# The second MLP product of an encoder layer: a fourth of its seven inner products is itself split into seven, and the row differences that this needs are made where the rows are made

## The chip, the cores and the metric

The kernel runs on one core of one Trainium2 chip. The metric is the device time of one execution in microseconds (us); the lower the better. The times shown are those of several runs of the kernel; the profile is one more execution, recorded by the hardware profiler. The engines of the core are TensorE (PE; its weight loads are listed as PEld), VectorE (DVE), ScalarE (ACT), GpSimd (POOL) and SyncE (SP, which here issues nearly all DMAs).

## The reference

One layer of an encoder over 2048 rows of 1024 numbers, float32. Attention with an output projection comes first (its code is not touched here and is left out), then the MLP:

```python
x = x + gt1 * (mixed @ w_o[l])
h = rmsnorm(x, g_norm2[l]) * (1.0 + sc2) + sh2
x = x + gt2 * (jnp.square(jax.nn.relu(h @ w1[l])) @ w2[l])
```

`w1` is 1024 x 4096 and `w2` is 4096 x 1024. `gt2` is a vector over the 1024 columns, and the last line's result is the output.

## The kernel before

Everything is computed transposed: columns of the reference lie on the 128 partitions, rows of the sequence along the free axis, in four blocks of 512 (`TB`). Float32 products are made of three matmuls each (`mm3`): every operand is split into a high part, cast by ACT, and a low part, the remainder, subtracted by DVE (`operand`, `split`); high x high, high x low and low x high are added up in PSUM. So each operand tile costs an ACT cast and a DVE subtraction before PE can use it. Since one helper records PE's and SP's instructions in the order of the program, all lines of the profile carry its line, L42, and work is told apart by tile names.

**The MLP's products are split into seven.** Both matrices are cut into 2 x 2 blocks, and seven products of sums of blocks take the place of eight products of blocks (the Strassen-Winograd scheme). They are numbered 1, 6, 5, 7, 2, 3, 4; 1, 2 and 4 take blocks as they are, 5, 6, 3 and 7 sums and differences of blocks. The rows are worked on in two halves: `mb` 1 first, then `mb` 0, each with two blocks of 512 rows (`odd` 1 and 0).

**Steps.** The MLP is a list of steps (`steps`), run in order; a step issues its matmuls. Before step n runs, the jobs that were put down for n with `at(n, job)` are issued (loads, sums), and the operands of later steps are prepared as long as no more than 8 operand tiles are in use (`ready - used + nxt.tiles <= 8`). `later.add(k, job)` issues a job k steps later. DVE, ACT and POOL then take their instructions in an order that a scheduler makes of the program; PE's and SP's stay as written.

- `Mixed`: the last eight steps of the attention's output projection (tiles `pso`, weights `wo`), while the first four groups of MLP input rows (`right_blocks`, tiles `cy`, `h`) are normalised, summed and split by ACT and DVE.
- `First(mb, j, i)`, the first product: 16 pairs of hidden blocks j by seven products i, 12 matmuls a step. `fetch` makes the four sums of the weight tile `w1` of pair j (tiles `ts`, and one in place in `w`), on DVE. `run` ends with the four hidden blocks and the sums of them that the second product needs, and `keep(i, src)` stores each of the seven to DRAM (`scr_hid[mb, i, ...]`). The steps of `mb` 1 also make the sums of `w2` (`second_sums`, tiles `w2s`, kept in `scr_s`).
- `Second(mb, i, j)`, a *plain* product of the second matrix: products 1, 6, 5 and 7 (`PLAIN`), each for `mb` 1 and `mb` 0, in 16 steps of 12 matmuls into four PSUM banks (tiles `oph`, `opv`, both from `hw`). `out` gathers the results, and `update` adds them, times `gt2`, into the rows (`scr_x`; tiles `txu`, `cxu`).
- `Outer(i, q, k)`, a *doubled* product: products 2, 3 and 4 are each split once more into seven, over both halves `mb`, in 7 x 8 steps of 6 matmuls (tiles `opr`, `ol`, from `r` and `l`). The left sides are sums of `w2`, made by `outer_sums` during `First` of `mb` 0 and kept in `scr_t`. The right sides are the stored rows: `half` loads four of them (1, 5, 3, 2; 5 and 3 from `mb` 0, 1 and 2 from `mb` 1), and `half_sum` makes four sums on DVE (5, 6, 7, 4), in tiles of 128 x 1024. `end` adds a finished bank into rows `txo`, loaded by `load_x` one step into the inner product that needs them.

**Order of the tail before:** plain 1, plain 6, doubled 2, plain 5, doubled 3, plain 7, doubled 4, all for `mb` 0 where plain. `plan` says at which steps a doubled product's right sides are loaded and summed; these lie in the products ahead of it. Plain loads (`hw`) stand 7 steps ahead, those behind a doubled product up to 12.

The inner order of a doubled product is 1, 5, 6, 3, 7, 2, 4. The sixth (2) completes the rows of block "11" and the seventh (4) those of block "21"; the PSUM bank of the seventh is free when DVE has added it into its rows.

## Time and profile before

| | us |
|---|---|
| median of 3 runs | 2572.12 (2569.36 to 2574.5) |
| the profiled execution | 2573.75 |
| its span in the trace | 2572.0 |
| mean granted PE clock | 0.998 of full speed |

The stages of the MLP in the trace, with the columns PE, weight loads, DVE, ACT, POOL (busy us, number of instructions), granted clock, DMA share, GB/s: plain 1 and 6 of `mb` 0, doubled 2, plain 5, doubled 3, plain 7, doubled 4.

```profile
2161.00:2250.00 89.00, 89.00 (x394) 73.69 (x393) 65.69 (x91) 41.83 (x74) 0.00 (x0) 1.00 0.80 304
2250.00:2326.00 76.00, 75.53 (x334) 62.19 (x332) 68.74 (x105) 49.84 (x86) 0.00 (x0) 1.00 0.69 249
2326.00:2371.00 45.00, 44.38 (x196) 36.71 (x197) 33.63 (x47) 18.91 (x33) 0.00 (x0) 1.00 0.63 234
2371.00:2448.00 77.00, 75.69 (x334) 62.30 (x332) 70.36 (x107) 49.87 (x86) 0.00 (x0) 1.00 0.74 261
2448.00:2492.00 44.00, 43.55 (x192) 36.07 (x193) 35.13 (x50) 18.29 (x32) 0.00 (x0) 1.00 0.66 261
2492.00:2568.00 76.00, 75.85 (x332) 61.51 (x330) 62.87 (x100) 45.95 (x79) 0.00 (x0) 1.00 0.43 146
```

An instruction's row gives its start, its time, the engine, what it writes and reads, and in brackets how long the engine stood idle before it and what ended that. Such idle time matters only on the engine that sets the end.

### The profile page before, as it was taken

The numbers are of one execution on the slowest core, as the hardware profiler recorded it, in microseconds if no ns is written. First come the engines' busy times: TensorE is split into PE (matmuls) and PEld (weight loads), VectorE is DVE, ScalarE is ACT, GpSimd is POOL, SyncE is SP. The second block draws the span as 40 slices with busy tenths as digits, with TensorE's granted clock in tenths as the row PEclk, the third lists the DMA queues.
The fourth block names the chain that finished last, engine by engine and source line by source line (L and its number), as shares of the span: only waits on it lengthen the run. The fifth ranks groups of instructions, "written<-read, shape, count | busy, mean of one in ns | idle before, by whom it ended". The sixth has DMA issues, their size and how long they took to land.

```text
span 2572.0 us, 39296 instructions
## 1 busy us (share of the span) xinstructions
PE 2542.0 (99%) x12484; PEld 2115.9 (82%) x12484; DVE 1965.5 (76%) x3433; ACT 1483.7 (58%) x2849; POOL 747.3 (29%) x1128
## 2 busy tenths in 40 slices
PE   9999999999999999999999999999999999999999
PEld 7888888888888888887887888888888888888877
DVE  7656767887789879998767777678776765797987
ACT  6323435667866686666745555566455555464645
POOL 4330144776776667776610000000000000000000
PEclk9999999999999999999999999999999999999999
DMA  9879879788977788756786887787677866766763
GB/s 356 331 296 364 338 282 291 215 239 280 277 245 229 239 280 269 245 189 204 224 317 227 288 286 272 261 303 252 216 253 257 262 233 243 301 245 239 260 259 127
DMA packets 276943, 674.80 MB, mean 262 GB/s; under 512 B 29952, under 2 KB 75008, under 8 KB 266112
## 3 DMA queue, kind: packets, MB, share of 16 engines
q1 hardware_dynamic: 275440, 667.57, 75.7%
q10 hardware_dynamic: 1296, 4.72, 0.5%
q8 instruction: 99, 1.62, 0.3%
q14 instruction: 108, 0.88, 0.1%
HBM read 461.93 MB, written 210.24 MB: 261 GB/s over the span
## 4 chain that ended last, share of the span: by engine, by line
PE 85%; DVE 6%; DMA 3%; ACT 2%; issue 2%; POOL 1%; SPq 1%; DVEq 0%; POOLq 0%; ACTq 0%
PE ps L42 30%; PE ps_s L42 12%; PE pt L42 11%; PE acc L42 6%; PE wt L42 6%; PE po L42 4%; PE pf L42 4%; PE z L42 4%; PE pq L42 3%; PE cz L42 2%; DVE p L42 2%; PE pso L42 1%; DVE opr L42 1%; DMA txo<-scr_x 1%; PE ct L42 1%
## 5 line engine op out<-in xcount | busy, mean ns | idle before, releaser
L42 PE MATMUL ps<-h,opw 128*128 128x512 f32 x1512 | 358.6, 389 | 0.0
L42 ACT CAST wth<-wt 128x512 fp32r<-128x512 f32 (+3 forms) x544 | 257.5, 484 | 174.0 <-PE wt L42 164.0
L42 PE MATMUL ps<-oph,opv 128*128 128x512 f32 x1536 | 349.7, 389 | 2.9 <-DVE txo L42 2.9
L42 POOL TENSOR_TENSOR b<-p 128x512 f32<-128x512 f32 (+1 forms) x320 | 292.5, 914 | 167.9 <-DVE p L42 90.4
L42 PEld LDWEIGHTS ps<-oph,opv 128*128 128x128 f32 x1536 | 288.1, 188 | 63.8 <-DVE txo L42 3.7
L42 DVE TENSOR_TENSOR wtl<-wt,wth 128x512 fp32r<-128x512 f32 (+3 forms) x544 | 290.5, 545 | 59.6 <-ACT wth L42 57.1
L42 PEld LDWEIGHTS ps<-h,opw 128*128 128x128 f32 x1512 | 283.6, 188 | 58.9
L42 PE MATMUL pt<-w,ht 128*128 128x512 f32 x1248 | 288.2, 391 | 0.0
L42 PE MATMUL ps_s<-h,opw 128*128 128x512 f32 x1152 | 277.0, 389 | 0.0
L42 PEld LDWEIGHTS pt<-w,ht 128*128 128x128 f32 x1248 | 232.9, 188 | 47.7
L42 DVE TENSOR_TENSOR_SCAN p<-z,p,zero 128x512 f32<-128x512 f32 x192 | 245.6, 1280 | 25.8 <-ACT z L42 18.4
L42 PEld LDWEIGHTS ps_s<-h,opw 128*128 128x128 f32 x1152 | 216.1, 188 | 44.9
L42 PE MATMUL acc<-wth,v 128*128 128x512 f32 (+3 forms) x544 | 220.7, 410 | 0.0
L42 ACT ACTIVATE z<-z 128x512 f32<-128x512 f32 (+1 forms) x320 | 166.5, 521 | 55.2 <-PE z L42 49.3
L42 PE MATMUL z<-k,q 128*128 128x512 f32 (+3 forms) x640 | 185.6, 371 | 7.7 <-DVE p L42 7.2
L42 PE MATMUL acc<-wtl,v 128*128 128x512 f32 (+3 forms) x544 | 185.7, 348 | 0.0
L42 PE MATMUL wt<-ident,b 128*128 128x128 f32 x1088 | 171.4, 273 | 1.0 <-DVE cols L42 0.3
L42 PEld LDWEIGHTS wt<-ident,b 128*128 128x128 f32 x1088 | 136.3, 140 | 42.1 <-DVE cols L42 1.8
L42 POOL TENSOR_TENSOR e<-e,cols 128x640 f32<-128x640 f32 (+4 forms) x128 | 143.0, 1123 | 84.9 <-DVE cols L42 57.0
L42 PE MATMUL po<-fx,ow 128*128 128x512 f32 x576 | 161.7, 393 | 0.5 <-DMA ow<-scr_wo 0.5
L42 DVE TENSOR_TENSOR opw<-w,opw 128x512 fp32r<-128x512 f32 x127 | 87.3, 691 | 95.0 <-ACT opw L42 95.0
L42 ACT CAST opr<-r 128x512 fp32r<-128x512 f32 x168 | 104.4, 623 | 83.6 <-PE ps L42 46.9
(211 smaller groups left out, 4761.8 us busy)
## 6 DMA issues: line engine op xcount, KB each, us to landing
q<-scr_q SPq DMA_DIRECT2D x128, 256.0 KB, 4.9
w<-in_w_dram SPq DMA_DIRECT2D x64, 512.0 KB, 5.7
hw<-scr_hid SPq DMA_DIRECT2D x64, 512.0 KB, 6.2
k<-scr_k SPq DMA_DIRECT2D x240, 128.0 KB, 4.3
v<-scr_v SPq DMA_DIRECT2D x120, 256.0 KB, 4.1
wa<-in_w_ada_dram SPq DMA_DIRECT2D x48, 512.0 KB, 6.6
ow<-scr_wo SPq DMA_DIRECT2D x24, 1024.0 KB, 6.6
hw<-scr_s SPq DMA_DIRECT2D x48, 512.0 KB, 7.2
```

What stands on the lines that cost most here:

```text
L42: return lambda *x, **y: self.tc.keep_in_program_order(f(*x, **y))
```

## The change

1. Product 7 becomes a doubled product. `PLAIN` loses it, and a new list `DOUBLE` is (7, 2, 3, 4); `scr_t` and `outer_sums` get it as a fourth, the latter now over all 16 pairs j. The tail becomes plain 1, doubled 7, plain 6, doubled 2, plain 5, doubled 3, doubled 4. Product 7 enters two blocks of rows, so an `Outer` of it adds each finished bank into twice as many rows, and writes half of them back to `scr_x`.
2. The first of the four half sums (5) goes. Instead, in `First` of `mb` 0 and for j < 8, `other` loads the row of `mb` 1 that was stored before (tiles `to`, 128 x 512), `keep` subtracts it from the new row on DVE, and the difference is stored two steps later.
3. For `mb` 1 and j < 2, `fetch` makes its four sums on POOL instead of DVE.
4. `update` is rewritten for the rows that product 7 no longer completes, stores of `end` go through `later.add(2, ...)`, and the steps in `plan`, of the plain loads and of `outer_sums` move.

```diff
-    PLAIN = (1, 6, 5, 7)
+    PLAIN = (1, 6, 5)
+    DOUBLE = (7, 2, 3, 4)
...
-    scr_t = {(i, pr): dram.tile([P, HP, CN], F32, name=f"scr_t{i}_{pr}") for i in (2, 3, 4) for pr in (3, 5, 6, 7)}
+    scr_t = {(i, pr): dram.tile([P, HP, CN], F32, name=f"scr_t{i}_{pr}") for i in DOUBLE for pr in (3, 5, 6, 7)}
...
-                    d[pr] = column_sum(dve, d["21"] if pr == 7 else temp(f"s{self.nm}_{pr}"), d[a], d[b], op)
+                    d[pr] = column_sum(pool if self.mb and self.j < 2 else dve, d["21"] if pr == 7 else temp(f"s{self.nm}_{pr}"), d[a], d[b], op)
...
             def keep(self, i, src):
-                sp.dma_start(scr_hid[self.mb, i, self.j // 2][:, self.j % 2, :], src)
+                dst = scr_hid[self.mb, i, self.j // 2][:, self.j % 2, :]
+                o = First.others.pop((self.mb, self.j, i), None)
+                if o is None:
+                    sp.dma_start(dst, src)
+                    return
+                column_sum(dve, o, src, o, ALU.subtract)
+                later.add(2, lambda: sp.dma_start(dst, o))
+
+            def other(self, i):
+                o = First.others[self.mb, self.j, i] = temp(f"o{self.nm}_{i}")
+                sp.dma_start(o, scr_hid[1, i, self.j // 2][:, self.j % 2, :])
...
                 if i == 5:
-                    d["v", n] = column_sum(dve, kept(f"v{self.nm}_{n}"), ps, d["s", n], ALU.add)
-                if i == 7:
                     column_sum(dve, d["s", n], ps, d["s", n], ALU.add)
-                    x = d["x", 1, 1, n]
-                    weigh(x, ps, HK + n)
-                    sp.dma_start(rows_of(out, mb, HK + n, 0), x)
...
             if i == 5:
-                update(mb, 0, 0, "v", spread(11, 12, 13, 14), spread(16, 17, 18, 19))
-            if i == 7:
-                update(mb, 1, 0, "v", spread(4, 5, 6, 7), spread(9, 10, 11, 12), False)
-                update(mb, 1, 1, "s", spread(10, 11, 12, 13), spread(16, 17, 18, 19))
+                update(mb, 1, 1, spread(1, 2, 3, 9), spread(6, 7, 8, 13))
...
+                if mb:
+                    update(mb, 0, 0, spread(11, 11, 11, 11), spread(16, 16, 17, 17), slot)
+                    update(mb, 1, 0, spread(13, 13, 14, 14), spread(18, 18, 19, 19), kept)
+                else:
+                    update(mb, 0, 0, spread(11, 12, 13, 14), spread(16, 17, 18, 19))
+                    update(mb, 1, 0, spread(15, 16, 17, 21), spread(20, 21, 22, 25), None, True)
...
-                for b, last in {5: (("22", 0),), 6: (("12", 0),), 3: (("12", 1),), 7: (("22", 1),), 2: (("11", 1),), 4: (("21", 1),)}.get(pr, ()):
-                    x = Outer.outs[b, n]
-                    mb, row, odd = self.place(b, n)
-                    weigh(x, ps, row)
-                    if last:
-                        sp.dma_start(rows_of(out, mb, row, odd), x)
+                for b, done in {5: (("22", 0),), 6: (("12", 0),), 3: (("12", 1),), 7: (("22", 1),), 2: (("11", 1),), 4: (("21", 1),)}.get(pr, ()):
+                    for x, mb, row, odd, last in Outer.outs[b, n]:
+                        weigh(x, ps, row)
+                        if done:
+                            dst = rows_of(out, mb, row, odd) if last else scr_x[2 * mb + odd, row]
+                            later.add(2, lambda dst=dst, x=x: sp.dma_start(dst, x))
...
-            x, y = {5: (5, 1), 6: (3, 5), 7: (6, 1), 4: (2, 6)}[pr]
-            t = hop[g].tile([P, 2, TB], F32, tag=f"h{pr}_{g}", name=f"r{i}_{pr}_{g}") if pr != 5 else halves[5, g]
+            x, y = {6: (3, 5), 7: (6, 1), 4: (2, 6)}[pr]
+            t = hop[g].tile([P, 2, TB], F32, tag=f"h{pr}_{g}", name=f"r{i}_{pr}_{g}")
...
-                elif j < 12:
-                    outer_sums((2, 3, 4)[j // 4], j % 4, begin + 7 * j + 9)
+                else:
+                    outer_sums(DOUBLE[j // 4], j % 4, begin + 7 * j + 5)
+                    if j < HP:
+                        for i, n in ((3, 2), (2, 5), (7, 2), (4, 5)):
+                            at(begin + 7 * j + n, lambda i=i, f=f: f.other(i))
...
-                at(begin - 1, steps[begin + 7].fetch)
+                for m, n in enumerate((-1, -1, 1, 2)):
+                    at(begin + n, lambda m=m, f=steps[begin + 7]: f.fetch(m))
...
-        plain_loads(f, 7)
-        plain_loads(plain(0, 6), 7)
-        plan = {"load": {1: (f + 1, 3), 5: (f + 2, 3), 3: (f + 13, 2), 2: (f + 21, 2)}}
-        plan["sum"] = {5: (f + 6, 3), 6: (f + 17, 2), 7: (f + 20, 2), 4: (f + 25, 2)}
-        for i, p in ((2, 5), (3, 7), (4, None)):
+        plain_loads(f, [])
+        e = len(steps)
+        plan = {"load": {1: (f - 5, 1), 5: (f - 1, 1), 3: (f + 4, 2), 2: (f + 18, 2)}}
+        plan["sum"] = {6: (f + 9, 2), 7: (f + 13, 2), 4: (f + 44, 2)}
+        for i, p in ((7, 6), (2, 5), (3, None), (4, None)):
             f = outer(i, plan)
+            e = len(steps)
             if p:
-                plain_loads(plain(0, p), 12)
-            e = f + 7 * HP
+                plain_loads(plain(0, p), [12, 11, 11, 11, 9, 8])
             plan = {"load": {1: (f + 6, 2), 5: (f + 17, 2), 3: (f + 30, 2), 2: (f + 46, 2)}}
-            plan["sum"] = {5: (f + 23, 2), 6: (f + 36, 2), 7: (e + 2, 2), 4: (e + 5, 2)}
+            plan["sum"] = {6: (e + 1 if i == 7 else f + 38, 2), 7: (e + 4, 2), 4: (e + 8, 2)}
```

How this moves instructions at three places. In the names, the first number after the letters is `mb` or the product, the last one a buffer.

First, DVE at the end of the output projection, before (`cy` and `h` are the MLP's input rows, `ts` and `w1` the weight sums of pair 0, `cxr` a row of the projection's result):

```order
L42 TENSOR_TENSOR cy1_3_12_17323<-cy1_3_22_17327,cy1_3_12_17323 128x512
L42 TENSOR_TENSOR ts1_0_1_5_17452<-w1_1_0_17449 128x512
L42 TENSOR_TENSOR ts1_0_1_6_17454<-ts1_0_1_5_17452,w1_1_0_17449 128x512
L42 TENSOR_TENSOR ts1_0_1_3_17456<-w1_1_0_17449,ts1_0_1_6_17454 128x512
L42 TENSOR_TENSOR w1_1_0_17449<-w1_1_0_17449 128x512
L42 SCALAR_TENSOR_TENSOR cxr0_2_17358<-pso0_2_17424,mod_258,cxr0_2_17358 128x512
L42 TENSOR_TENSOR h1_5_3_17418<-cy1_3_11_17321,h1_5_3_17418 128x512
L42 TENSOR_TENSOR cy1_3_22_17327<-cy1_3_22_17327,cy1_3_11_17321 128x512
```

DVE at the same place with the change:

```order
L42 TENSOR_TENSOR cy1_3_12_17327<-cy1_3_22_17331,cy1_3_12_17327 128x512
L42 SCALAR_TENSOR_TENSOR cxr0_2_17362<-pso0_2_17428,mod_258,cxr0_2_17362 128x512
L42 TENSOR_TENSOR h1_5_3_17422<-cy1_3_11_17325,h1_5_3_17422 128x512
L42 TENSOR_TENSOR cy1_3_22_17331<-cy1_3_22_17331,cy1_3_11_17325 128x512
L42 TENSOR_TENSOR h1_7_3_17426<-cy1_3_12_17327,h1_7_3_17426 128x512
L42 TENSOR_TENSOR cy1_3_21_17329<-cy1_3_21_17329,cy1_3_22_17331 128x512
```

The four sums, which need the loaded weight tile, no longer stand among the row operations; they and those of pair 1 are now POOL's, which has nothing else between the attention and the norms:

```order
L42 TENSOR_TENSOR os1_7_0_16735<-o1_6_0_16696,os1_7_0_16735 128x512
L42 TENSOR_TENSOR ts1_0_1_5_17456<-w1_1_0_17453 128x512
L42 TENSOR_TENSOR ts1_0_1_6_17458<-ts1_0_1_5_17456,w1_1_0_17453 128x512
L42 TENSOR_TENSOR ts1_0_1_3_17460<-w1_1_0_17453,ts1_0_1_6_17458 128x512
L42 TENSOR_TENSOR w1_1_0_17453<-w1_1_0_17453 128x512
L42 TENSOR_TENSOR ts1_1_1_5_17512<-w1_1_1_17509 128x512
L42 TENSOR_TENSOR ts1_1_1_6_17514<-ts1_1_1_5_17512,w1_1_1_17509 128x512
```

Second, SP where a doubled product passes to a plain one. Before, from doubled 2 to plain 5 (`txo2_11` are the rows that its sixth inner product completes, `txo2_21` those of its seventh; `hw` are loads of the plain product, `r` one of the next doubled one):

```order
L42 DMA out_0_dram<-txo2_11_0_25500 128x512
L42 DMA out_0_dram<-txo2_11_1_25502 128x512
L42 DMA hw0_5_2_25590<-scr_hid0_5_1_16801 128x1024
L42 DMA hw0_5_2_25590<-scr_s4_1_16921 128x1024
L42 DMA r3_2_1_25593<-scr_hid1_3_5_16853 128x1024
L42 DMA txo2_21_0_25604<-scr_x3_2_214 128x512
L42 DMA txo2_21_1_25606<-scr_x3_3_215 128x512
```

With the change, from doubled 7 to plain 6:

```order
L42 DMA r2_2_1_25087<-scr_hid1_2_5_16849 128x1024
L42 DMA scr_x3_4_216<-cxo7_11_01_24992 128x512
L42 DMA out_0_dram<-cxo7_11_00_24994 128x512
L42 DMA scr_x3_5_217<-cxo7_11_11_24996 128x512
L42 DMA out_0_dram<-cxo7_11_10_24998 128x512
L42 DMA txo7_21_01_25102<-scr_x3_6_218 128x512
L42 DMA txo7_21_00_25104<-scr_x2_6_210 128x512
L42 DMA txo7_21_11_25106<-scr_x3_7_219 128x512
L42 DMA txo7_21_10_25108<-scr_x2_7_211 128x512
```

Four stores and four loads stand where two and two did, and no other load stands between them.

Third, DVE with the change in the second inner product of doubled 4, which now follows doubled 3 (`opr`, `ol` are operands, `r4` half sums):

```order
L42 TENSOR_TENSOR opr4_5_3_27397<-r4_5_1_26858,opr4_5_3_27397 128x512
L42 TENSOR_TENSOR opr4_5_4_27410<-r4_5_2_26883,opr4_5_4_27410 128x512
L42 TENSOR_TENSOR ol4_5_4_27413<-l4_5_0_27272,ol4_5_4_27413 128x512
L42 TENSOR_TENSOR r4_4_0_27416<-r4_2_0_27193,r4_6_0_27091 128x1024
L42 TENSOR_TENSOR r4_7_2_27418<-r4_6_2_27145,r4_1_2_26750 128x1024
L42 TENSOR_TENSOR opr4_5_5_27428<-r4_5_2_26883,opr4_5_5_27428 128x512
L42 TENSOR_TENSOR opr4_5_6_27441<-r4_5_3_26906,opr4_5_6_27441 128x512
L42 TENSOR_TENSOR ol4_5_6_27444<-l4_5_0_27272,ol4_5_6_27444 128x512
L42 TENSOR_TENSOR r4_4_1_27447<-r4_2_1_27218,r4_6_1_27116 128x1024
L42 TENSOR_TENSOR r4_7_3_27449<-r4_6_3_27168,r4_1_3_26776 128x1024
```

Before, these eight half sums of doubled 4 stood in plain 7, between its operands `oph` and `opv`.

More of the change, by code (lines that the diff above doesn't have):

```diff
@@ L1441, in encoder_kernel @@
         class First(Step):
-            pair = {}
+            pair, others = {}, {}
             def __init__(self, mb, j, i):
@@ L1618, in rows_of, with update @@
             return t[n * P : (n + 1) * P, tb * TB : (tb + 1) * TB]
-        def update(mb, r, odd, acc, loads, adds, keep=True):
-            d = Second.whole
+        def update(mb, r, odd, loads, adds, home=None, last=False):
+            xs = {}
             def fetch(n):
-                d["x", r, 1 - odd, n] = x = (temp if keep else kept)(f"xu{mb}_{r}{odd}_{n}")
+                xs[n] = x = (home or temp)(f"xu{mb}_{r}{odd}_{n}")
                 sp.dma_start(x, scr_x[2 * mb + odd, HK * r + n])
             def add(n):
-                x = d["x", r, 1 - odd, n]
-                weigh(x, d[acc, n], HK * r + n)
-                if keep:
-                    later.add(3, lambda: sp.dma_start(scr_x[2 * mb + odd, HK * r + n], x))
+                x, row = xs[n], HK * r + n
+                weigh(x, Second.whole["s", n], row)
+                dst = rows_of(out, mb, row, odd) if last else scr_x[2 * mb + odd, row]
+                later.add(3, lambda: sp.dma_start(dst, x))
             for n in range(HK):
@@ L1643, in plain, with slot @@
             if i == 6:
[L1644 removed]
+                update(mb, 0, 1, spread(0, 1, 2, 8), spread(4, 5, 6, 12))
             if i == 5:
[L1646 to L1649 removed]
+                update(mb, 1, 1, spread(1, 2, 3, 9), spread(6, 7, 8, 13))
+                wide = []
+                def slot(nm):
+                    if not wide:
+                        t = raw_pair([P, HK, TB], F32, nm)
+                        wide.extend(t[:, n, :] for n in range(HK))
+                    return wide.pop(0)
+                if mb:
[4 more added lines that the diff above has]
+                    update(mb, 1, 0, spread(15, 16, 17, 21), spread(20, 21, 22, 25), None, True)
             return f
@@ L1937, in encoder_kernel @@
             later.tick()
+        later.flush()
 def _lay_out(i):
```

27 lines of the change are left out of this document (14 added, 13 removed).

## The prediction

> **What bounds the kernel now.** I read the page first, then the windows of 20 us, then the timeline at the few places where TensorE (PE) did not run, and last the chain of waits.
>
> ```profile
> span 2572.0 us, 39296 instructions
> PE 2542.0 (99%) x12484; PEld 2115.9 (82%) x12484; DVE 1965.5 (76%) x3433; ACT 1483.7 (58%) x2849; POOL 747.3 (29%) x1128
> ...
> PE 85%; DVE 6%; DMA 3%; ACT 2%; issue 2%; POOL 1%; SPq 1%; DVEq 0%; POOLq 0%; ACTq 0%
> ```
>
> PE is busy for 99% of the span and carries 85% of the chain that ended last. So a matmul that goes saves its issue time, and any other engine counts only where it makes PE wait. The issue time stands in the chain of waits, in a stretch of the doubled product 4:
>
> ```profile
> 2318.59 7.13 DMA txo<-scr_x
> ...
> 2546.09 10.88 PE ps L42 x48
> ```
>
> 48 matmuls in 10.88 us are 0.2267 us each (the 389 ns of a matmul's row overlap). A 20 us window with PE never idle therefore holds 88 to 90 matmuls, and the MLP shows few others:
>
> ```profile
> 1340.00:1360.00 20.00, 20.00 (x90) 16.57 (x89) 17.65 (x29) 12.45 (x21) 0.00 (x0) 1.00 0.98 359
> 1360.00:1380.00 20.00, 16.02 (x57) 12.20 (x56) 16.93 (x27) 8.16 (x15) 0.00 (x0) 0.83 0.33 124
> ...
> 2280.00:2300.00 20.00, 20.00 (x90) 16.54 (x89) 20.00 (x30) 12.66 (x22) 0.00 (x0) 1.00 0.25 80
> ...
> 2320.00:2340.00 20.00, 18.92 (x84) 15.31 (x83) 14.35 (x22) 9.01 (x16) 0.00 (x0) 1.00 1.02 395
> ...
> 2440.00:2460.00 20.00, 18.23 (x81) 14.78 (x80) 13.96 (x22) 9.18 (x16) 0.00 (x0) 1.00 1.01 383
> ```
>
> The columns are PE, weight loads, VectorE (DVE), ScalarE (ACT), GpSimd (POOL), PE's granted clock, the DMA share and GB/s. Three places lose matmuls: where the output projection gives way to the first MLP product (1360 to 1380, 57 matmuls, clock 0.83), and where a doubled product gives way to a plain one (2320 and 2440).
>
> **Part 1: fewer matmuls.** A plain product of the second MLP matrix takes 16 steps x 4 x 3 = 192 matmuls for each half of the rows, 384 for both; a doubled one takes 7 x 8 x 2 x 3 = 336. Product 7 goes from the one to the other: 48 matmuls less, 48 x 0.2267 = **-10.9 us**. PE's work is otherwise unchanged.
>
> **Part 2: eight weight sums go from DVE to POOL at the start of the first product.** The timeline of before:
>
> ```profile
> 1344.69 21.47 PE L42 MATMUL pso<-opm,wo 128*128 128x512 f32 x94
> ...
> 1359.23 0.68 DVE L42 TENSOR_TENSOR cy<-cy,cy 128x512 f32<-128x512 f32 x1
> ...
> 1362.85 0.69 DVE L42 TENSOR_TENSOR ts<-w 128x512 f32<-128x512 f32 x1 [2.94 <-DMA w<-in_w_dram]
> ...
> 1364.91 0.68 DVE L42 TENSOR_TENSOR w<-w 128x512 f32<-128x512 f32 x1
> ...
> 1367.49 0.62 ACT L42 CAST h<-cy 128x512 fp32r<-128x512 f32 x1 [6.93 <-DVE cy L42]
> ...
> 1369.89 1.22 PE L42 MATMUL ps<-h,opr 128*128 128x512 f32 x2 [3.73 <-ACT opr L42]
> ...
> 1371.35 7.67 PE L42 MATMUL ps<-h,opr 128*128 128x512 f32 x22 [0.24 <-DVE opr L42]
> ```
>
> DVE works in order. It waits 2.94 us for the weight tile, makes four sums, and only then goes on with the rows (cy) for which ACT has waited 6.93 us; ACT's casts of the first weights (opr) stand behind those. PE ends the projection at 1344.69 + 21.47 = 1366.16, waits 3.73 us, and its next 22 matmuls take 7.67 us, 0.35 us each: the clock is down too. Two steps of 12 matmuls should end at 1366.16 + 24 x 0.2267 = 1371.60; they end at 1371.35 + 7.67 = 1379.02. The place costs 7.4 us.
>
> Afterwards DVE has neither the wait nor the sums there. Its rest up to the first opr: 1359.9, when its row work stopped, plus six row operations and two residuals, 8 x 0.69, is 1365.4, and the two operands follow at 1366.1 and 1366.8; the first is what PE needs at 1366.16. POOL takes 1.04 us for an operation of this size:
>
> ```profile
> L42 POOL TENSOR_TENSOR b<-p 128x512 f32<-128x512 f32 x224 | 233.4, 1042 | 155.2 <-DVE p L42 87.0 <-PE wt L42 17.9 <-PE z L42 16.9
> L42 DVE TENSOR_TENSOR w<-wr,w 128x512 fp32r<-128x512 f32 x64 | 39.4, 683 | 0.2
> L42 DVE TENSOR_TENSOR opr<-r,opr 128x512 fp32r<-128x512 f32 x168 | 113.3, 686 | 23.9 <-ACT opr L42 22.0
> ```
>
> So the sum that the second operand needs is there at 1362.85 + 1.04 = 1363.9, and the fourth at 1367.0; its operand is wanted on PE four steps of 2.72 us after 1366.2. The other four sums belong to steps from 1385 on. The bounds are 0 (the stall stays) and -7.4 us; I take **-7.4**, since every wait in that chain leads to what is taken away.
>
> Two rules of the Trainium skill bear on it. "TensorE: Matmul & The Clock Gate", Part 1, has the array at half clock after an idle window of about 3.4 us until a busy one has passed; the 3.73 us of idle, the 0.35 us a matmul and the clock of 0.83 agree, and by it the slow 22 matmuls go with the wait. "GPSIMD Engine Reference", section 1, has GpSimd's SBUF interface shared with VectorE, with contention when a VectorE instruction has two SBUF inputs, which these row operations have. By that rule the sums on POOL would hold up the very rows that PE waits for, which is the first rival below. The row w<-wr,w (two SBUF inputs, from 100 to 400 us, where POOL works too) has 683 ns against 686 with POOL silent, so the trace speaks against it and I charge nothing.
>
> **Part 3: what the tail does.** The tail becomes plain 1, doubled 7, plain 6, doubled 2, plain 5, doubled 3, doubled 4. Before, the two losses there have one form:
>
> ```profile
> 2313.13 11.04 PE L42 MATMUL ps_s<-opr,ol 128*128 128x512 f32 x48
> ...
> 2315.30 1.40 DVE L42 SCALAR_TENSOR_TENSOR txo<-ps,mod,txo 128x512 f32<-128x512 f32 x2
> ...
> 2318.59 1.02 SPq L42 DMA_DIRECT2D txo<-scr_x x2
> ...
> 2325.81 1.41 DVE L42 SCALAR_TENSOR_TENSOR txo<-ps_s,mod,txo 128x512 f32<-128x512 f32 x2 [1.16 <-DMA txo<-scr_x]
> ...
> 2326.62 13.71 PE L42 MATMUL ps<-oph,opv 128*128 128x512 f32 x59 [1.08 <-DVE txo L42]
> ...
> 2448.45 13.90 PE L42 MATMUL ps<-oph,opv 128*128 128x512 f32 x60 [1.77 <-DVE txo L42]
> ```
>
> PE ends the sixth of seven inner products at 2313.13; DVE, behind with half sums, adds it into the rows (txo) 2.2 us later; SP, in order, stores those rows before it loads the last ones; these land 7.13 us later (the chain's row above), and until DVE has added into them a PSUM bank is taken that the plain product needs. From 2313.13 to PE's return are 13.5 us; eight steps and six matmuls, 10.9 + 1.4, cover 12.2. The two places cost 1.08 + 1.77 = 2.85 us.
>
> At 7 to 6 there are twice as many rows: two more additions (1.40 us a pair) before the stores, one more (0.7) before the bank is free: +2.1. But the half sums of the next product now stand in plain 6, so DVE is not behind (up to -2 of its 2.2), and the loads come straight behind the stores, with no three other loads between (0.5 us each by the row of two: about -1.5): 12.1 to 14.1, a wait of 0 to 1.9 us. At 2 to 5 four of eight half sums are gone, and the three loads too: 10.0 to 12.0 us, no wait. Doubled 3 to 4 is new. In the second inner product of 4 DVE has 12 operand subtractions and 8 half sums:
>
> ```profile
> 2299.88 1.13 DVE r L42
> 2301.02 1.20 DVE opr L42 x2
> ```
>
> 12 x 0.60 + 8 x 1.13 = 16.2 us beside 10.9 us of PE: 5.3 us late, against operands made up to 8 tiles, 5.3 steps or 7.3 us, ahead. That is a wait of 0 to 2 us. Together 0 to 3.9 us instead of 2.85: -2.9 to +1.1; if DVE is no earlier than before, +4 more. I take **0**.
>
> **Part 4: extra work that should be covered.** In the first product of the second half of the rows DVE gets 32 subtractions of 128x512 more (22.0 us at the 0.686 of the row above) and 16 more weight sums (11.0); the half sums that the former replace, 12 x 1.13, go from the tail. The stretch has 30% of DVE free:
>
> ```profile
> 1862.00:2014.00 152.00, 152.00 (x672) 125.84 (x672) 106.54 (x169) 81.65 (x144) 0.00 (x0) 1.00 0.77 255
> ...
> 1540.00:1560.00 20.00, 20.00 (x90) 16.57 (x89) 15.46 (x26) 12.33 (x23) 0.00 (x0) 1.00 0.87 309
> ```
>
> In its first 152 us DVE would go from 106.5 to about 128 us. DMA gets 4 x 0.262 MB per 19 us more: 255 + 55 = 310 GB/s, which the second row, from the first product of the other half of the rows, carries with 90 matmuls. Operands stand up to 8 steps, 21 us, ahead of PE there. Cost **0**; without that cover every late microsecond would count, up to 33 us (below).
>
> **Sum.** The profiled execution took 2573.75 us, 1.75 around its span. 2573.75 - 10.9 - 7.4 + 0 = 2555.4 on its scale; the median of the runs shown is 1.6 lower: 2572.1 - 18.3 = **2554 us**.
>
> **Rivals.**
> - *The stall at the first product stays* (POOL's sums or a later row of DVE's chain hold the casts): for it speaks that DVE's new arithmetic leaves under 1 us of slack at 1366.16; against it that 6.9 us of ACT's wait go. If POOL's four sums, 4 x 1.04 us, held DVE's rows up for as long, PE would again wait some 4 us and start slowly. Then 2572.1 - 10.9 - 0 to 2 = about 2561. Chance 0.15.
> - *The tail waits more*: the double rows at 7 to 6 and the two doubled products in a row. A wait of over 3.7 us would bring the slow clock too, 2.7 us as in part 2: two such places 2 x 4 + 2.7 less the 2.85 of before, +8: 2562. Chance 0.13.
> - *Slower*: the DMA queue can't carry the first product's extra loads. At 255 GB/s a period of 84 matmuls, 19.0 us, moves 4.85 MB now; 4.85 + 1.05 need 23.1 us, for 8 periods +33 us: 2587. It decides once loads land later than the 21 us of cover. The 309 GB/s above speak against it. Chance 0.05.
> - *No change*: the first two together and more waits in the tail, 2570. Chance 0.04. That the change would not do what it says is excluded for PE, whose order has 48 matmuls fewer.
>
> **How the numbers follow.** The forecast has 0.63, with its own range 2551 to 2557. The first two rivals, 0.28, lie up to 2562; the range to 2564 takes them in, and 2550 below allows the tail's -2.9. This kernel's runs can tell about 0.2%, 5 us: below 2567 is faster, 0.63 + 0.15 + 0.13 = 0.91; same 0.04; slower 0.05.
>
> **What would show it.** Part 1: 12436 matmuls where the page had 12484, at the same 10.88 us per 48. Part 2: the window 1360 to 1380 with 88 to 90 matmuls at clock 1.00, and no PE wait for opr; a PE wait there of 3 us or more makes it wrong. Part 3: PE's waits for txo at the two places 0 to 2 us. Part 4: no PE wait for opw between 1840 and 2140. Wrong is the whole if PE's waits in the tail exceed 8 us or a DMA of the new loads ends DVE's waits often.

## The result and the profile after

| | us, median (range, runs) | ratio to before, 95% interval |
|---|---|---|
| before, beside it | 2571.79 (2569.36 to 2574.75, 12) | |
| changed | 2570.43 (2564.17 to 2572.88, 12) | 0.9990 (0.9981 to 0.9999) |
| forecast | 2554 (2550 to 2564) | |

The median is 1.4 us lower. That is less than the 0.2% that the forecast named as what these runs can tell, so it counts as no change, although the interval just leaves out 1. The profiled executions took 2573.75 us before and 2568.92 us after, with spans of 2572.0 and 2567.2 us. The head of the page of the changed kernel:

```profile
span 2567.2 us, 39419 instructions
PE 2534.1 (99%) x12436; PEld 2109.1 (82%) x12436; DVE 2012.0 (78%) x3501; ACT 1496.2 (58%) x2871; POOL 760.8 (30%) x1136
```

PE is as busy as before, 99% of the span, and issues 12436 matmuls, 48 fewer, as forecast. So 10.9 us went, and most of it was given back. Where, the windows of 20 us show (columns as in the prediction: PE, weight loads, DVE, ACT, POOL, clock, DMA share, GB/s):

```profile
1360.00:1380.00 20.00, 16.82 (x67) 13.44 (x66) 17.94 (x19) 9.13 (x16) 13.33 (x8) 0.91 0.70 263
...
2100.00:2120.00 20.00, 16.39 (x60) 12.99 (x59) 7.61 (x12) 7.17 (x13) 0.00 (x0) 0.83 0.95 348
...
2240.00:2260.00 20.00, 17.46 (x71) 13.94 (x70) 14.01 (x21) 6.69 (x13) 0.00 (x0) 0.91 1.03 380
...
2500.00:2520.00 20.00, 19.63 (x83) 15.09 (x82) 20.00 (x29) 11.92 (x21) 0.00 (x0) 1.00 0.22 74
```

A full window has 90 matmuls; each one missing is 0.2267 us. The first place still lacks 23 (5.2 us; before 33, 7.5 us). The second, where the first product gives way to plain product 1, is new: 30 lacking, 6.8 us. The third, 7 to 6, lacks 19 (4.3 us), the fourth, in doubled product 4, lacks 7 (1.6 us). The passage 2 to 5 (2360 to 2380) is full, with 90. Together 17.9 us; the three places of before lacked 33, 6 and 9, 10.9 us. So -10.9 + 7.0 = -3.9 us, against -4.8 us between the two spans. About 0.5 us of the rest lies ahead of the MLP: PE's last matmul of the output projection ends at 1366.2 us in the profile of before and at 1365.6 in this one. These sums hold for the two profiled executions; the medians lie only 1.4 us apart. PE's waits from 1340 us on, without one of 0.3 us (us in total, times, longest):

```profile
PE ps L42 <- ACT cp L42: 3.6, 1, 3.6
PE ps_s L42 <- ACT ps_s L42: 3.2, 1, 3.2
PE ps L42 <- DVE txo L42: 2.5, 1, 2.5
```

Three waits, 9.3 us, and slow clock behind each.

**The start of the first product.** From the timeline, POOL, DVE, ACT and PE:

```profile
1362.67 1.80 POOL L42 TENSOR_TENSOR ts<-w 128x512 f32<-128x512 f32 x1 [59.04 <-ACT h L42]
...
1374.58 1.73 POOL L42 TENSOR_TENSOR w<-w 128x512 f32<-128x512 f32 x1
1363.90 1.12 DVE L42 TENSOR_TENSOR opr<-w,opr 128x512 fp32r<-128x512 f32 x1
...
1370.26 6.60 DVE L42 TENSOR_TENSOR opw<-w,opw 128x512 fp32r<-128x512 f32 x4
1372.98 0.62 ACT L42 CAST opw<-ts 128x512 fp32r<-128x512 f32 x1 [0.67 <-POOL ts L42]
1373.62 0.57 ACT L42 COPY ps_s<-ps 128x512 f32<-128x512 f32 x1
1365.46 5.60 PE L42 MATMUL ps<-h,opr 128*128 128x512 f32 x24
1374.24 4.21 PE L42 MATMUL ps_s<-h,opw 128*128 128x512 f32 x12 [3.18 <-ACT ps_s L42]
```

The wait for opr is gone: PE goes straight on at 1365.46. But POOL needs 1.6 to 1.8 us a sum instead of 1.04 and ends at 1376.3; DVE's four subtractions beside it take 1.65 us each instead of 0.69. ACT works in order: its copy of the sum bank (ps_s<-ps), which PE needs for its third step, stands behind a cast that waits for POOL's sixth sum. PE waits 3.18 us two steps later than before.

**The end of the first product.** SP, ACT and PE:

```profile
2091.99 4.76 SPq L42 DMA_DIRECT2D scr_t<-wt  x2
2096.80 1.91 SPq L42 DMA_DIRECT2D wt<-in_w_dram  x4
2099.23 0.47 SPq L42 DMA_DIRECT2D hw<-scr_hid  x1
2105.40 0.62 ACT L42 CAST oph<-hw 128x512 fp32r<-128x512 f32 x1 [6.11 <-DMA hw<-scr_hid]
2106.55 0.58 ACT L42 COPY cp<-ps 128x512 f32<-128x512 f32 x1
2107.18 5.49 PE L42 MATMUL ps<-h,opw 128*128 128x512 f32 x12 [3.61 <-ACT cp L42]
```

With 16 instead of 12 groups of weight sums, SP has the sums' stores and loads in its order up to the end of the product. It waits there for DVE's sums, and only at 2099.23 issues the first load (hw) of plain product 1. ACT has a cast of that tile in its order ahead of the copy that frees a PSUM bank; it stands 6.11 us, and PE 3.61. Before, where this product ended at 2160.8 us, the last such store was issued by 2100.8, and the same load stood 14.7 us ahead of its cast, which waited for nothing:

```profile
2130.98 0.45 SPq L42 DMA_DIRECT2D hw<-scr_hid  x1
2145.69 0.61 ACT L42 CAST oph<-hw 128x512 fp32r<-128x512 f32 x1
```

**7 to 6.** The last rows of product 7 are loaded behind the stores of the rows before them:

```profile
2234.49 4.61 SPq L42 DMA_DIRECT2D txo<-scr_x  x4
2244.06 2.73 DVE L42 SCALAR_TENSOR_TENSOR txo<-ps_s,mod,txo 128x512 f32<-128x512 f32 x4 [2.41 <-DMA txo<-scr_x]
2245.52 12.80 PE L42 MATMUL ps<-oph,opv 128*128 128x512 f32 x48 [2.54 <-DVE txo L42]
```

The chain of waits has the first of these loads, issued at 2234.49:

```profile
2234.49 9.48 DMA txo<-scr_x
```

It landed after 9.48 us; in the profile of before, from doubled 2 to plain 5, it was 7.13 us.

### The profile page after: what moved, and what is told of

Read it like the earlier page. It is cut to its first block, busy times and chain, and to the rows that moved or that the text cites. A ratio compares the mean times of both kernels' runs of the same rounds, so it can differ in the third digit from the quotient of the medians.

```text
span 2567.2 us, 39419 instructions
## 1 busy us (share of the span) xinstructions
PE 2534.1 (99%) x12436; PEld 2109.1 (82%) x12436; DVE 2012.0 (78%) x3501; ACT 1496.2 (58%) x2871; POOL 760.8 (30%) x1136
## 4 chain that ended last, share of the span: by engine, by line
PE 86%; DVE 5%; ACT 3%; DMA 2%; issue 2%; POOL 1%; SPq 1%; DVEq 0%; POOLq 0%; ACTq 0%
PE ps L42 29%; PE ps_s L42 14%; PE pt L42 11%; PE acc L42 6%; PE wt L42 6%; PE po L42 4%; PE z L42 4%; PE pf L42 4%; PE pq L42 3%; PE cz L42 2%; DVE p L42 2%; PE pso L42 1%; DVE opr L42 1%; PE ct L42 1%; ACT z L42 1%
## 5 line engine op out<-in xcount | busy, mean ns | idle before, releaser
L42 PE MATMUL ps<-oph,opv 128*128 128x512 f32 x1152 | 263.8, 391 | 2.5 <-DVE txo L42 2.5
L42 PEld LDWEIGHTS ps<-oph,opv 128*128 128x128 f32 x1152 | 217.2, 189 | 48.4 <-DVE txo L42 3.0
L42 ACT CAST opr<-r 128x512 fp32r<-128x512 f32 x224 | 139.3, 623 | 107.7 <-PE ps L42 51.1
L42 PE MATMUL ps<-opr,ol 128*128 128x512 f32 x768 | 176.4, 389 | 0.1
L42 DVE TENSOR_TENSOR opr<-r,opr 128x512 fp32r<-128x512 f32 x224 | 151.2, 688 | 27.5 <-ACT opr L42 24.8
L42 PEld LDWEIGHTS ps<-opr,ol 128*128 128x128 f32 x768 | 144.0, 188 | 30.5 <-DVE ol L42 0.4
```

The costliest lines, as they stand in the source:

```text
L42: return lambda *x, **y: self.tc.keep_in_program_order(f(*x, **y))
```

## The experiments

My theory after these views: three separate waits, each with a cause of its own in the order of one engine, took the gain of the 48 matmuls. At the start POOL and DVE shut each other out of SBUF, so that the move of eight sums only exchanged one wait for another. The rivals: the sums were a full success and the rest went elsewhere; the waits share one cause (DMA, or DVE late on the whole), so that mending one shows the next.

### Each part alone

The sums back on DVE (e1):

```diff
-column_sum(pool if self.mb and self.j < 2 else dve, ...
+column_sum(dve, ...
```

> The changed kernel with the eight weight sums of its first two weight pairs back on VectorE, everything else as changed. Theory (the sums on GpSimd and VectorE's subtractions with two SBUF inputs run one after the other, so that the move to GpSimd only exchanged one wait for another): the wait of 3 to 4 us for opr returns, the window 1360 to 1380 has 57 to 60 matmuls instead of 67, and the time is 1 to 3 us above the changed kernel, about 2572. Rival 1 (the move was worth all of the 7.4 us forecast, and the forecast failed elsewhere): about 2577 to 2578. Rival 2 (the move was worth nothing): within 0.5 us.

Measured: 2571.39 us (2565.86 to 2576.34, 11 runs), ratio 1.0000 (0.9991 to 1.0009). That is 1.0 us above the changed kernel, less than the runs can tell, and the window 1360 has 66 matmuls, not 57 to 60: PE waits 2.52 us for opr in this execution. So rival 1 is out; between the theory and rival 2 this run does not decide. The weight tile landed early here, which run e7 below shows to matter.

Only the second pair back on DVE (e2):

```diff
-pool if self.mb and self.j < 2 else dve
+pool if self.mb and self.j < 1 else dve
```

> The changed kernel with only the first weight pair's four sums on GpSimd, the second pair's four on VectorE. Theory (GpSimd and VectorE exclude each other on SBUF): GpSimd is done about 1369.5 instead of 1376, VectorE's operand subtractions after that go from 1.65 back to 0.69 us, at the price of four sums of 0.69, ScalarE's copy of the sum bank no longer stands behind casts that wait for GpSimd, and PE's wait of 3.2 us falls under 1 us; 3 to 5 us faster than the changed kernel. Rival (VectorE is simply the full engine there, wherever the sums are made): the 2.8 us of sums on VectorE delay the operands by as much, the wait stays 2 to 4 us, time within 1 us.

Measured: 2567.13 us (2563.4 to 2570.55, 11), ratio 0.9980 (0.9971 to 0.9989): 3.3 us below the changed kernel, whose interval overlaps this one a little. From the timeline of this run:

```profile
1371.32 2.49 DVE L42 TENSOR_TENSOR opw<-w,opw 128x512 fp32r<-128x512 f32 x4
1372.16 3.02 PE L42 MATMUL ps_s<-h,opw 128*128 128x512 f32 x12 [1.41 <-ACT ps_s L42]
```

POOL, with four sums, is done at 1368.3, and DVE's four subtractions behind it take 2.49 us instead of 6.60. PE's wait fell from 3.18 to 1.41, not quite under 1, and the clock stayed at 1.00. The theory holds: the second pair on POOL cost more than it gave.

The first loads of plain product 1 earlier (e3):

```diff
-plain_loads(f, [])
+plain_loads(f, [11, 10, 9, 8])
```

> The changed kernel with the first four loads of plain product 1 (second half of the rows) issued 4, 3, 2 and 1 steps earlier in SyncE's order, so that the first stands ahead of the stores that wait for VectorE. Theory (PE's wait of 3.61 us at 2107 comes from this one load, late in SyncE's order, for which ScalarE waits in order ahead of the copy that frees a PSUM bank): the load is issued by 2093 and has landed by 2100, ScalarE no longer waits 6 us for it, PE's wait goes under 0.5 us, the window 2100 to 2120 has 87 to 90 matmuls instead of 60: 5 to 6.5 us faster. Rival (the DMA share of 0.95 at 380 GB/s there is the limit, so an earlier load makes a later one late): the wait moves to another load or store and less than 1.5 us is gained.

Measured: 2563.88 us (2560.96 to 2564.24, 5), ratio 0.9966 (0.9954 to 0.9979), 6.6 us below the changed kernel. SP's queue and the window:

```profile
2089.31 0.45 SPq L42 DMA_DIRECT2D hw<-scr_hid  x1
```

```profile
2100.00:2120.00 20.00, 20.00 (x90) 16.57 (x89) 10.50 (x18) 11.52 (x21) 0.00 (x0) 1.00 0.99 351
```

The first load is issued 9.9 us sooner, ahead of the stores that wait; only it and the three loads behind it were moved, the DMA share is as high as in the changed kernel (0.99), and PE does not stop. The 6.8 us of this place came from the order of these loads.

The last rows of product 7 earlier (e4):

```diff
-at(f + HP * OUTER.index(pr) + 1, ...load_x(b))
+at(f + HP * OUTER.index(pr) + (-6 if (i, pr) == (7, 4) else 1), ...load_x(b))
```

> The changed kernel with the last four row loads of doubled product 7 issued seven steps earlier in SyncE's order, ahead of the stores of the rows before them. Theory (PE's wait of 2.54 us for txo at 2245 is the latency of these loads, issued behind the stores): no wait for txo, the window 2240 to 2260 has 86 to 90 matmuls instead of 71, 2.5 to 4 us faster. Rival (VectorE, behind with half sums, or the PSUM bank it frees is the limit, and the DMA share of 1.03 there makes some other load late): 1 us or less.

Measured: 2565.22 us (2562.68 to 2568.63, 7), ratio 0.9976 (0.9965 to 0.9987), 5.2 us below the changed kernel; the window 2240 has 88 matmuls and no wait for txo. The gain is above the 4.3 us of the place. Part of it is chance elsewhere: the window 1360, where nothing was edited, has 78 matmuls at clock 1.00 in this profile and 67 at 0.91 in the one above (PE's wait was 2.51 and 3.18 us).

### Together, and what is left

The three edits at once (e5):

> The three edits of the runs before together: second weight pair's sums on VectorE, the first four loads of plain product 1 earlier, the last row loads of doubled product 7 earlier. Theory (three separate waits, each with its own cause): their gains add, 2570.4 - 3.3 - 6.6 - 5.2 = about 2555 to 2557, and the windows 2100 and 2240 have 86 to 90 matmuls at once. Rival (the waits share a cause, such as DMA or VectorE being late on the whole, so that mending one brings out another): 2560 or more, with a new wait elsewhere in the second product.

Measured: 2560.17 us (2558.67 to 2560.59, 5), ratio 0.9952 (0.9939 to 0.9964). The windows 2100 and 2240 have 90 and 89 matmuls at once, so these two waits are mended independently of each other. But the sum is 10.3 us below the changed kernel instead of 15.1, which is where the rival had put the time, and a small part of the rival holds: the window 2140 to 2160, in plain 1, lacks 3 to 9 matmuls (0.7 to 2.0 us) in e3 and in every run from e5 to e10, and at most two in the changed kernel, e1, e2 and e4. ACT waits there for loads of plain 1, and PE in this run 0.58 us for ACT. So mending the passage brings out a smaller loss behind it. How much of the other missing gain is chance in the single runs, as named under e4, is not shown.

Then ACT's order at the start (e6, with the three edits):

```diff
-ready - used + nxt.tiles <= 8
+ready - used + nxt.tiles <= (5 if n == KT else 8)
...
-for m, n in enumerate((-1, -1, 1, 2)):
+for m, n in enumerate((0, 0, 1, 2)):
```

> The three edits, and at the first step of the first product operands made up to 5 tiles ahead instead of 8, so that in ScalarE's order the copy of the sum bank stands ahead of the second pair's three casts; the second pair's sums on VectorE go behind the first pair's five operand subtractions. Theory (what is left of PE's wait for the copy, 1.41 us with the second pair on VectorE, is ScalarE's order): that wait falls under 0.5 us, 1 to 1.5 us faster than the three edits alone. Rival (the casts ahead of the copy wait for GpSimd's fourth sum of the first pair anyway, since GpSimd's sums take 1.7 us each beside VectorE): the wait stays above 1 us, no difference over 0.5 us.

Measured: 2559.61 us (2557.52 to 2561.22, 5), ratio 0.9951 (0.9939 to 0.9964): 0.6 us, which these runs can't tell from nothing. PE's wait for ps_s is 1.06 us: the rival, the casts ahead of the copy wait for POOL's fourth sum.

With that, the first pair on DVE too (e7; the diff of e1 on top of e6):

> As the run with three edits and 5 tiles ahead, but the first pair's four sums on VectorE too, none on GpSimd. Theory (GpSimd's sums and VectorE's subtractions take turns, so that GpSimd still takes about 4 x 1.04 us of VectorE's time where VectorE itself would need 4 x 0.69): the window 1360 to 1380 has about as many matmuls as with the first pair on GpSimd, within 4, time within 1.5 us. Rival (GpSimd's sums are a real relief of VectorE's chain of row operations, as forecast): VectorE's sums come ahead of the rows, PE waits 2.5 us or more for opr and starts slowly, 3 to 6 us slower than with them on GpSimd.

Measured: 2566.15 us (2562.17 to 2568.41, 7), ratio 0.9975 (0.9963 to 0.9986), 6.5 us above e6. My theory fell; the rival, which is the forecast's own reason, was right. The two timelines can be laid side by side, since the load of the weight tile was issued at 1355.5 us in both and the first sum began at the same time. With the first pair on POOL (e6):

```profile
1363.75 1.61 POOL L42 TENSOR_TENSOR ts<-w 128x512 f32<-128x512 f32 x1 [58.97 <-PE pso L42]
1364.80 1.12 DVE L42 TENSOR_TENSOR opr<-w,opr 128x512 fp32r<-128x512 f32 x1
1366.14 5.60 PE L42 MATMUL ps<-h,opr 128*128 128x512 f32 x24
```

With it on DVE (e7):

```profile
1363.80 0.69 DVE L42 TENSOR_TENSOR ts<-w 128x512 f32<-128x512 f32 x1 [4.18 <-DMA w<-in_w_dram]
1371.56 0.69 DVE L42 TENSOR_TENSOR opr<-w,opr 128x512 fp32r<-128x512 f32 x1
1370.84 1.22 PE L42 MATMUL ps<-h,opr 128*128 128x512 f32 x2 [4.49 <-ACT opr L42]
```

On DVE the first operand comes 7.8 us after the first sum begins, which waits for the tile (in e1 the sums began at 1361.02 and the operand at 1368.79); DVE's rows wait for it behind the sums. On POOL the rows are done while the tile is still under way. So the first pair on POOL is worth a wait of 4.49 us and its slow clock, and the landing time, which differs by 2.8 us between e1 and e7, counts for less.

Half sums of product 4 later (e8, on top of e6):

```diff
-7: (e + 4, 2), 4: (e + 8, 2)
+7: (e + (14 if i == 3 else 4), 2), 4: (e + (24 if i == 3 else 8), 2)
```

> The three edits, 5 tiles ahead, and in doubled product 4 the eight half sums begin 10 and 16 steps later. Theory (the window 2500 to 2520 loses 4 to 7 matmuls because VectorE is full there with operand subtractions and half sums): 88 to 90 matmuls there, 1 to 1.5 us faster than without the last edit, about 2553 to 2555. Rival (the operands of the third inner product are late for another reason, such as its loads): the window still has 84 matmuls and the time stays.

Measured: 2560.56 us (2557.89 to 2563.4, 5), ratio 0.9955 (0.9943 to 0.9968), no gain over e6. The window 2500 to 2520 has its 90 matmuls, and the next one is:

```profile
2520.00:2540.00 20.00, 19.63 (x84) 15.28 (x84) 20.00 (x31) 12.06 (x22) 0.00 (x0) 1.00 0.37 111
```

The place is mended and the loss stands 20 us later: DVE is full over the whole of product 4, and the half sums have to go somewhere. The cause was named rightly, the cure only moves it.

### The first product's own rows

In the first product of the second half DVE now waits for a store in most of the first eight periods. Its waits between 1840 and 2100 us in the changed kernel (none of this kind before):

```profile
DVE ts L42 <- DMA scr_hid<-to: 17.4, 6, 3.3
```

A weight sum (ts) takes over the buffer of a first difference (to) and must wait until that has been stored. PE did not wait for DVE there in this profile, but it did in six of the eight profiles of e1 to e8, 0.8 to 3.6 us in all. Two ways to shorten it, both on top of e6: eight buffers for these tiles (e9), and the store one step earlier (e10):

```diff
-name="tp", bufs=7 ... name="accp", bufs=12
+name="tp", bufs=8 ... name="accp", bufs=11
```

> The run with three edits and 5 tiles ahead, with 8 instead of 7 buffers for the short-lived rows (ts, to) and 11 instead of 12 for the kept ones. Theory (in the first product of the second half VectorE waits about 3 us in each of the first eight periods for the store of a first difference, since a weight sum takes over its buffer; this makes VectorE late and lets PE wait 0 to 3 us in all, differently in each execution): VectorE's waits for scr_hid<-to between 1840 and 2000 fall from 17 us to under 5 us, no PE wait for cp there, 0.5 to 1.5 us faster. Rival (the eleven kept buffers hold up doubled product 7, whose rows need twelve): a new wait of 1 us or more at 2200 to 2260, no gain.

```diff
-later.add(2, lambda: sp.dma_start(dst, o))
+later.add(1, lambda: sp.dma_start(dst, o))
```

> The run with three edits and 5 tiles ahead, with the stores of the first differences one step of 2.72 us earlier in SyncE's order. Theory (as in the run with eight buffers): VectorE's waits for scr_hid<-to fall from 17 us to about 5 us or less, no PE wait for cp between 1840 and 2000, 0.5 to 1.5 us faster. Rival (the store stands now ahead of the subtraction's end, so SyncE waits for VectorE and its later loads are late): SyncE's loads of w and wt come later, new VectorE waits for them, no gain or up to 2 us slower.

Measured: 2556.48 us (2554.66 to 2558.93, 5), ratio 0.9937 (0.9925 to 0.9950), and 2556.57 us (2555.22 to 2558.43, 5), ratio 0.9940 (0.9927 to 0.9954). Both are some 3 us below e6, and neither has a PE wait for cp there, but DVE's waits for the stores stayed, 16.6 and 15.7 us. PE's waits in e10 from 1360 us on, without one of 0.3 us:

```profile
PE ps L42 <- ACT opv L42: 0.7, 1, 0.7
PE ps L42 <- DVE opr L42: 0.6, 1, 0.6
```

So the step in between was not as I had it (17 to 5 us or less), and why both gain is open: the intervals of e6 and these two overlap, and one profile without a wait does not show that there never is one. In e6's profile the two windows with these waits (1920 to 1960) lack 8 matmuls, 1.8 us; in e9 and e10 none is missing there. These are the fastest versions here, faster than before and than the changed kernel.

### The sums on POOL, by themselves

The kernel before with the move of the eight sums alone (e11):

> The kernel before with nothing changed but the eight weight sums of the first two pairs moved to GpSimd. Theory (the sums on GpSimd take turns with VectorE, and ScalarE's copy of the sum bank stands behind casts of the second pair's sums): the wait of 3.7 us for opr goes, one of about 3 us for ps_s comes, 1 to 3 us faster than before, about 2569 to 2571. Rival (the move alone brings the 7.4 us of the forecast, and only the new products spoil it): about 2564.

Measured: 2570.23 us (2567.28 to 2572.26, 11), before 2571.14, ratio 0.9994 (0.9985 to 1.0003). The wait for opr went from 3.73 to 0.57 us, one of 2.20 us for ps_s came. What part 2 put at 7.4 us brings 0.9 us, not distinguishable from none. The profile of this run, one of the fastest of its eleven, shows more: the window 1360 to 1380 has 75 matmuls instead of 57, 4.1 us.

Sums of four pairs on POOL, to see the same instructions where nothing starts up (e12, the changed kernel with `self.j < 4` in the place of `self.j < 2`):

> The changed kernel with the sums of the first four weight pairs on GpSimd instead of the first two, so that eight more of them fall where nothing starts up. Theory (GpSimd and VectorE take turns on SBUF, one whole instruction each): a subtraction of VectorE with two SBUF inputs that meets a sum goes from 0.69 to about 0.69 + 1.04 = 1.7 us, additions that read PSUM (cp<-ps,cp) and ScalarE's casts keep 0.69 and 0.62, a sum that meets nothing takes about 1.04 us. Rival (the lengthening at the start comes from the DMA traffic or from the row loads there): between 1380 and 1430 VectorE's subtractions stay at 0.69 to 0.8 beside GpSimd's sums. Either way PE has enough ahead there, and the time stays within 3 us of the changed kernel.

Measured: one run, 2566.38 us. POOL and DVE in the fourth pair's period:

```profile
1401.97 1.29 POOL L42 TENSOR_TENSOR ts<-w 128x512 f32<-128x512 f32 x1 [14.70 <-DMA w<-in_w_dram]
1403.34 1.72 POOL L42 TENSOR_TENSOR ts<-ts,w 128x512 f32<-128x512 f32 x1
...
1406.72 1.29 POOL L42 TENSOR_TENSOR w<-w 128x512 f32<-128x512 f32 x1
1402.55 0.69 DVE L42 TENSOR_TENSOR cp<-ps_s,cp 128x512 f32<-128x512 f32 x1 [0.73 <-PE ps_s L42]
1403.21 0.69 DVE L42 TENSOR_TENSOR opw<-w,opw 128x512 fp32r<-128x512 f32 x1
1403.82 1.78 DVE L42 TENSOR_TENSOR w2s<-w2s 128x512 f32<-128x512 f32 x1
1407.60 0.97 DVE L42 TENSOR_TENSOR opw<-w,opw 128x512 fp32r<-128x512 f32 x1 [1.99 <-ACT opw L42]
```

Each instruction waits until the other engine's has ended. POOL's second sum begins at 1403.34, while DVE is in a subtraction until 1403.90, and ends 1.16 us after that. DVE's next, at 1403.82, begins inside that sum, which ends at 1405.06, and ends 0.54 us after it; the one at 1407.60 meets the rest of the last sum (until 1408.01) and ends 0.56 us after it. The addition that reads PSUM (1402.55) runs through inside a sum at 0.69. A sum that meets nothing takes 1.29 us, not the 1.04 expected. There is no start-up there and no row load, so the rival is out.

The two do not strictly alternate. At the start POOL's first sum meets DVE's row operations, which follow one another without a gap, and has to let several pass. The longest such case is in e8:

```profile
1361.36 4.23 POOL L42 TENSOR_TENSOR ts<-w 128x512 f32<-128x512 f32 x1 [56.17 <-PE pso L42]
1361.95 0.69 DVE L42 TENSOR_TENSOR cy<-cy,cy 128x512 f32<-128x512 f32 x1
```

Four row operations of DVE begin at 1361.95 to 1363.75, after the sum has begun, and each runs through. The sum ends at 1365.59, 1.15 us after the fourth is done, much as POOL's second sum above; the row operation behind the fourth is held, to 1.62 us. The first sum took 2.91 us in e2, 2.99 in e5 and 3.42 in e11 in the same way.

## Why the prediction was wrong, point by point

**Part 1** (-10.9 us) was right. The matmuls are 12436, and with the other waits mended (e10) the span is 2553.3 us. That is 18.7 under the 2572.0 of before. Of this, 10.9 are the matmuls; 2.3 are, as far as the profiles tell, chance: the output projection, whose matmuls are the same, ended at 1363.8 instead of 1366.2 us; and the rest is less loss in the MLP: the windows under 88 matmuls lack 23 in e10, 5.2 us, and 48 before, 10.9 us. e10's profile is also the fastest of its five runs.

**Part 2** (-7.4 us) is the first step that failed, at the sentence that charged nothing for POOL and DVE meeting. The step read the mean of w<-wr,w, 683 ns, "from 100 to 400 us, where POOL works too". What POOL works on there, the grouped view of before for these 300 us says; its costliest group is

```profile
L42 POOL TENSOR_TENSOR cy<-cv,mhalf 128x8 f32<-128x8 f32 x27 | 48.4, 1791 | 96.3 <-DVE cv L42 92.4 <-DVE aff L42 3.8
```

and none has more than 8 elements a partition, a few MEMSETs apart. A row that never met the thing cannot speak against it. e12 shows the thing itself, with the addition that reads PSUM left alone. The rule of the Trainium skill that the step set aside, "GPSIMD Engine Reference", section 1, was right; "SBUF — State Buffer", section "SBUF: two separate sides", says it in full, that the one that starts first holds the shared ports for the whole instruction and the other is blocked, which the rows of e12 agree with to within 0.2 us. That several of VectorE's operations can pass a sum that is already waiting, as in e8, it does not say.

The price of a sum was mis-sized in the same step. Taken from b<-p, 1.04 us; a row of before with two inputs of this size from SBUF, as these sums have,

```profile
L42 POOL TENSOR_TENSOR os<-o,os 128x512 fp32r<-128x512 f32 x32 | 41.4, 1292 | 7.6 <-ACT os L42 7.6
```

has 1.29, and in the changed kernel, beside DVE, it is 1.6 to 1.8. So the fourth sum was there at 1369.6, not 1367.0, and the eighth at 1376.3. The first half of the step did hold: DVE's rows were done in time (and where the tile comes early, as in e8, they pass ahead of POOL's sum), PE did not wait for opr, and four sums on POOL are worth 6.5 us of time once the rest is in order (e7 against e6). Four sums too many, and ACT's copy behind their casts, took it back. The step had set these aside with "The other four sums belong to steps from 1385 on". That is when PE uses them; but operands are made up to 8 tiles ahead, and so two of their casts stand in ACT's order at 1371.69 and 1372.98, ahead of the copy at 1373.62 that PE waits for. The forecast's first rival was of this kind, with casts held up, a wait of "some 4 us" and 2561, at 0.15; it looked for the wait at opr, and it came two steps later.

**Part 3** (0 us) was mis-sized at one place. At 7 to 6 it had "a wait of 0 to 1.9 us"; measured are 2.54 us and 1.76 us of slow clock behind it (48 matmuls in 12.80 us instead of 11.04), 4.3 us in the window. DVE was not behind, as it had said, and the load was issued 3.9 us after PE began the seventh inner product, against 5.5 before. The term that was mis-sized is the landing: the working kept the 7.13 us of before, and it took 9.48, so that DVE waits 2.41 us for the rows. Why it took longer is not shown; the DMA share, 1.03 here and 1.02 before, does not tell the two apart. 2 to 5 without a wait and 0 to 2 us in product 4 (1.6) were right. Net of the 3.4 us of the two windows of before, part 3 came to +2.5 us.

**Part 4** (0 us) is the other step that failed. It costed 32 subtractions, 16 sums and their bytes, and in the profile these are covered, as it said: PE's windows from 1840 to 2000 are full, at 311 GB/s and 126 of 160 us of DVE. In six of the next eight profiles they are not quite, with the waits for cp of 0.8 to 3.6 us named above. It left out what the additional work does in SP's order when the product ends. Four groups of sums, whose stores wait for DVE, now stand ahead of the first load of the next product; 3.61 us of wait and the slow clock behind it, 6.8 us in the window, and 6.6 us back in e3 by the place of the first loads. "No PE wait for opw between 1840 and 2140" named the right stretch, but not the wait: PE waited for the copy to cp that frees a PSUM bank, and in this profile never for opw.

Sum by sum: -10.9 as forecast, -2.3 in the place of -7.4, +2.5 for part 3, +6.8 for part 4: -3.9, where the profiled spans have -4.8 and the medians -1.4. The forecast's rival for no change, "the first two together and more waits in the tail", was nearest, at 0.04; the three waits lie at passages between products, where each depends on an order and not on an amount of work, and a sum of such misses should have been given far more. That the time itself came out at that rival's 2570 is luck: it had only "more waits in the tail", and the largest loss stands ahead of the tail.

## What to carry to other kernels

Where an edit adds work that is covered on average, follow the orders of the engines through the end of that stretch: a store that waits in a queue ahead of the next stage's first load, or a cast ahead of the copy that frees a PSUM bank, cost more here than all the work added. Before a row is used as evidence that two engines do not disturb each other, see that the large instructions of both really overlap there. Work moved to GpSimd paid here where it took a late input out of VectorE's order, and only for as many instructions as that needed.

## What the runs showed of the hardware that was not expected

- GpSimd and VectorE shut each other out by whole instructions when both read two SBUF inputs: 0.69 us became up to 1.78, and a sum of 1.29 mostly 1.6 to 1.8. They do not alternate: VectorE's operations that follow one another without a gap pass a waiting sum, which then took up to 4.23 us (e8). An addition with one input in PSUM kept 0.69 (e12).
- Short idle times cost the clock too. Behind 2.54 us of idle (7 to 6, above) 48 matmuls took 1.76 us longer, behind 3.18 us 24 took 1.8 us longer; behind 2.51 us in e4 and 2.15 us in e12 no more than 0.2 us was lost. "TensorE: Matmul & The Clock Gate" of the Trainium skill, Part 1, puts the window at about 3.4 us and free-running; that the same idle time sometimes costs (2.54 and 2.51 us) agrees with the second, while 2.54 us is shorter than the first.
- The same place in the same code differs from one execution to the next: PE's wait for ps_s at the start was 3.18, 3.76 and 2.51 us in the changed kernel, e3 and e4. With the slow clock that comes or not, this can by estimate spread the time by some 3 us at one place (1.25 us of wait and 1.8 us of slow clock). PE's last matmul of the output projection, which no edit touched, ended between 1363.8 and 1366.6 us in the fourteen profiles. The changed kernel's runs spread over 8.7 us, those of before over 5.4, and those of e9 and e10, five runs each, over 4.3 and 3.2.
